# A token-major x product and a convolution summed by accumulating DMAs in layer A of a two-layer decoder

## The chip, the core and the metric

The kernel runs on one core of a Trainium2 chip. Its time is the device time of one execution in microseconds (us); for the kernel before it is the median of 3 runs, 1240.77 us, between 1240.29 and 1242.27. The engines are called PE (matmul; PEld is its weight load), DVE (vector), ACT (scalar, activation functions), POOL (GpSimd) and SP (the queue that issues nearly all DMAs). Each engine runs its own instructions strictly in their written order and waits at an instruction until what it needs is there.

## The reference, cut to what matters

256 tokens, model width 2048, all in float32. Layer A is a Mamba-2 mixer; layer B, dilated window attention, isn't touched. Of layer A this matters:

```python
h = x * (1.0 + scale) + shift                      # 256 x 2048, scale and shift from ada_w
z, xBC, dt = split(h @ in_w, [4096, 4096 + 6144])  # xBC: 4096 columns x, 1024 B, 1024 C
xBC = silu(causal_depthwise_conv(xBC, conv_w, conv_b))   # 4 taps: y[t] = sum_j w[j] * x[t-3+j] + b
xs, B, C = split(xBC)                              # 8 groups: 512 columns of x, 128 of B, 128 of C
y = ssd(xs * dt, dt * A, B, C) + xs * D_skip       # one chunk of 256 tokens
y = rms_norm(y * silu(z)) * norm_g @ out_w
```

## The kernel before, in words

Every product is made exact enough by splitting: a weight piece of 512 KB (`raw`, 128x1024) is loaded by SP into one of six buffers, ACT copies it to a rounded `whi` (L126), DVE subtracts to get the rest `wlo` (L127), four buffers each, and PE multiplies whi by the high and low halves of the activation and wlo by the high half. There are two forms. In `tm_mults` (L217 to L219) the activation is the stationary side and the result has tokens on partitions (token-major): per 128 rows of the weight, six matmuls of 512 columns. In `cm_part` (L176, L178) the weight is stationary and the result has channels on partitions (channel-major): per 128 rows and 512 channels, four matmuls of 512 columns and four of 256. During the startup `cm_piece` (L162 to L165) does the channel-major product with twelve matmuls of 256 columns, because the high and low halves of h come into being one after the other.

The startup loads 32 MB of `ada_w` to make scale and shift (L299), and h, 128 channels at a time; meanwhile PE works on pieces of products for which part of h exists. Ten products are begun that way and their partial sums parked in tiles (`begun`, L371). The products of x and of B and C of group 0 run through the whole startup in PSUM.

Then come the groups g = 0 to 7. `product` makes z (token-major), x and every second time B and C for two groups (channel-major). With channels on partitions the convolution (`conv`, L377) is shifts along the free axis: ACT multiplies by the last tap and adds the bias (L381), DVE adds three taps (L384), ACT applies Silu (L386). For x this is done on four tiles of 128 channels per group, after the two halves of each have been joined by ACT and DVE (L425, L426). `stage1` makes decay factors (`seg`: a broadcast load into `cbc`, Relu L687, Exp L690, product with the scores L691), turns the group's x into token-major with eight PE transposes into PSUM (L699), and lets DVE scale it by dt, D and the decay (L701, L704, L709). `stage2` multiplies on PE (L721, L729), adds and gates (L730, L731); `stage3` normalizes. Sixteen `ada_w` columns for the gate are worked off between pieces (L299).

The order on each engine isn't the written one: `arrange` lists the work by a model (`price`, `forward`, `backward`) and writes the order found into the program. The model prices every instruction, buffers and DMA; what it decides here is where in ACT's and DVE's queues the convolution's steps stand among the splits of the weight pieces.

Of the kernel before, what the change touches and what calls it, by code (L numbers as in the profile page):

```python
# [11 lines left out]
F32 = mybir.dt.float32  # L12
# [8 lines left out]
P = 128  # L21
# [27 lines left out]
WSUB = [("xs", g) for g in range(1, G)] + [("bc", g) for g in (2, 4, 6)]  # L49
# [22 lines left out]
def trunk(ctx, tc, xT, x, ada0, par, cst, bias, lnrow, ada, wdt, win, wsub, wout, wkv, wk, wbin, wbout, out):  # L72
# [278 lines left out]
    with ExitStack() as cA:  # L351
# [14 lines left out]
        with ExitStack() as cS:  # L366
# [5 lines left out]
                     ("xs", 1): (win[5], 4, as_cm(y[0])), ("bc", 2): (win[1], 4, as_cm(y[1])),  # L372
                     ("z", 2): (win[14], 14, y[2]), ("bc", 4): (win[2], 12, as_cm(y[5])), ("z", 4): (win[16], 6, y[4]),
                     ("z", 3): (win[15], 12, y[3]), ("z", 6): (win[18], 10, y[6]), ("z", 5): (win[17], 8, y[7])}
            xs, bc, sz = {}, {}, dict(enumerate(szt))
# [29 lines left out]
            def product(kind, g, pre=None):  # L405

                src, k0, part = begun.get((kind, g), (None, 0, None))
                if src is None:
                    src = win[{"bc": g // 2, "xs": 4 + g, "z": 12 + g}[kind]]
                if kind == "z":  # L410
                    ps = tm_chunk(src, hh_, hl_, rate=R, k0=k0, pre=pre)
                    if g not in sz:
                        sz[g] = p0.tile([P, 2, 512], F32, name="sz")
                    for b in range(2):
                        if part is not None:
                            V.tensor_tensor(part[:, b, :], ps[b], part[:, b, :], op=ALU.add)
                        S.activation(sz[g][:, b, :], part[:, b, :] if part is not None else ps[b], AF.Silu)
                    return
# [12 lines left out]
                if kind == "xs":  # L431
                    xs_conv(g, t)
                else:
                    bc_conv(g, t)

            with ExitStack() as c0:
# [58 lines left out]
                pss = {-2: first[0], -1: first[1]}  # L495
# [85 lines left out]
                for i, (k, q, ends) in enumerate(order):  # L581
# [8 lines left out]
                    z = str(k)[0] == "z"  # L590
# [38 lines left out]
                xs_conv(0, tiles(first[1]))  # L629
# [37 lines left out]
            def stage1(g):  # L667
# [11 lines left out]
                for w in range(2):  # L679
                    h0 = g * HPG + 4 * w  # L680
                    cbc = px.tile([P, 4, 2, P], F32, name="cbc")
                    nc.sync.dma_start(cbc, bass.AP(tensor=cumd.tensor, offset=cumd.offset + h0 * L,
                                                   ap=[[0, P], [L, 4], [P, 2], [1, P]]))
                    seg = px.tile([P, 4, 2, P], F32, name="seg")
                    for hh in range(4):
                        for b in range(2):
                            m = S.activation(seg[:, hh, b, :], cbc[:, hh, b, :], AF.Relu,  # L687
                                             bias=cumT[:, b, h0 + hh:h0 + hh + 1], scale=-1.0)
                            PINS.append((m.ins.name, early.ins.name))
# [5 lines left out]
                xd = px.tile([P, 2, 512], F32, name="xd", bufs=1)  # L695
                for b in range(2):
                    px_ = aux.tile([P, 512], F32, name="aux")
                    for i in range(4):
                        T.transpose(px_[:, i * P:i * P + P], xs[g][:, i, b * P:b * P + P], ident)  # L699
                    heads = px_.rearrange("p (h e) -> p h e", h=HPG)  # L700
                    V.tensor_tensor(xd[:, b, :].rearrange("p (h e) -> p h e", h=HPG), heads,  # L701
                                    dtT[:, b, g * HPG:(g + 1) * HPG, None].to_broadcast([P, HPG, 64]),
                                    op=ALU.mult)
                    V.tensor_tensor(y[g][:, b, :].rearrange("p (h e) -> p h e", h=HPG), heads,  # L704
                                    dskip[:, g * HPG:(g + 1) * HPG, None].to_broadcast([P, HPG, 64]),
                                    op=ALU.mult)
                    if b == 0:
                        xo = px.tile([P, 512], F32, name="xo", bufs=1)
                        V.tensor_tensor(xo.rearrange("p (h e) -> p h e", h=HPG), heads,  # L709
                                        dec[:, 0, g * HPG:(g + 1) * HPG, None].to_broadcast([P, HPG, 64]),  # L710
                                        op=ALU.mult)
# [474 lines left out]
def graph(ins):  # L1186

    nodes, tiles, live, lastpe = [], {}, {}, {}
    for x in ins:
# [3 lines left out]
        v.i, v.e = len(nodes), "SP" if "DMA" in type(x).__name__ else str(x.engine).split(".")[1]  # L1193
# [66 lines left out]
def build(ins, pools):  # L1260
# [9 lines left out]
    for x in ins:  # L1270
        if type(x).__name__ != "BassTilePoolBoundary":
            continue
        if x.name in byalloc:
# [13 lines left out]
            for tg, a, b, bufs in mine:  # L1287
                near = [(o, a < d and c < b or not tilewise) for kk, o, c, d in seen if kk == k and base < d and c < at]
                rng[tg] = (a, b, bufs, [o for o, full in near if full], [o for o, full in near if not full])
            held[p.id] = [(k, tg, a, b) for tg, a, b, bufs in mine]  # L1290
# [387 lines left out]
def _layout(x, c, ada_w, ada_b, ln_g, ln_b, a_in_w, a_conv_w, a_conv_b, a_dt_bias,  # L1678
# [4 lines left out]
    def put(name, a):  # L1683
# [43 lines left out]
        "wsub": _pieces(np.concatenate([xs[:, 512:], bc[:, 512:]], 1), 256, 4),  # L1727
# [24 lines left out]
```

## Time and profile before

| what | value |
|---|---|
| time, median of 3 runs | 1240.77 us |
| profiled execution, its span | 1238.4 us (the runs' median is 2.4 us above it) |
| PE busy | 1227.6 us, 99% of the span |
| DVE, ACT, POOL busy | 84%, 57%, 0% |
| DMA | 334.47 MB, 270 GB/s over the span |
| startup, the part at 420 GB/s | about the first 160 us |
| groups of layer A | about 160 to 520 us |

An engine's busy time counts an instruction from start to modelled end; matmuls overlap, so PE's pace is read from the distance between starts. In the grouped lines, "x64 | 11.0, 273 | 0.0" means 64 instructions, 11.0 us busy, 273 ns each, and 0.0 us of idle time just before them.

### The profile page before, as it was taken

The numbers are of one execution on the slowest core, as the hardware profiler recorded it, in microseconds if no ns is written. First come the engines' busy times: TensorE is split into PE (matmuls) and PEld (weight loads), VectorE is DVE, ScalarE is ACT, GpSimd is POOL, SyncE is SP. The second block draws the span as 40 slices with busy tenths as digits, with TensorE's granted clock in tenths as the row PEclk, the third lists the DMA queues.
The fourth block names the chain that finished last, engine by engine and source line by source line (L and its number), as shares of the span: only waits on it lengthen the run. The fifth ranks groups of instructions, "written<-read, shape, count | busy, mean of one in ns | idle before, by whom it ended". The sixth has DMA issues, their size and how long they took to land.

```text
span 1238.4 us, 18082 instructions
## 1 busy us (share of the span) xinstructions
PE 1227.6 (99%) x6712; PEld 1058.1 (85%) x6712; DVE 1035.9 (84%) x1481; ACT 703.1 (57%) x1054; POOL 0.2 (0%) x4
## 2 busy tenths in 40 slices
PE   8999999999999999999999999999999999999998
PEld 8889888888888888888888888888888888888886
DVE  6999998989999999978888699998865746757677
ACT  4655466768948589864335455444446644444561
POOL 0000000000000000000000000000000000000000
PEclk9999999999999999999999999999999999999999
DMA  9999977656696855748998669999985563551671
GB/s 368 422 422 421 422 271 241 223 189 234 263 339 224 318 182 190 245 154 294 384 386 308 233 221 369 412 377 378 353 308 187 200 192 103 168 182 64 203 285 68
DMA packets 81743, 334.47 MB, mean 270 GB/s; under 512 B 9108, under 2 KB 9844, under 8 KB 69496
## 3 DMA queue, kind: packets, MB, share of 16 engines
q1 hardware_dynamic: 81656, 333.33, 73.8%
q8 instruction: 52, 0.85, 0.3%
q14 instruction: 35, 0.29, 0.1%
HBM read 331.11 MB, written 2.18 MB: 269 GB/s over the span
## 4 chain that ended last, share of the span: by engine, by line
PE 86%; DMA 11%; DVE 2%; ACT 1%; issue 0%; SPq 0%; ACTq 0%
PE acc L176 27%; PE acc L178 14%; PE acc L217 12%; PE acc L218 12%; PE acc L219 12%; DMA raw<-in_win 8%; DMA araw<-in_ada 2%; PE py L729 2%; PE aux L993 1%; PE aux L699 1%; PE po L1017 1%; PE po L1006 1%; PE aux L994 1%; PE aux L721 1%; DMA y<-in_ada 1%; PE aux L783 0%
## 5 line engine op out<-in xcount | busy, mean ns | idle before, releaser
L126 ACT ACTIVATE whi<-raw 128x1024 fp32r<-128x1024 f32 (+1 forms) x393 | 409.7, 1049 | 342.2 <-PE acc L176 131.6
L127 DVE TENSOR_TENSOR wlo<-raw,whi 128x1024 fp32r<-128x1024 f32 (+1 forms) x393 | 471.2, 1211 | 119.2 <-ACT whi L126 113.3
L176 PE MATMUL acc<-act,whi 128*128 128x512 f32 x1456 | 376.8, 395 | 0.0
L176 PEld LDWEIGHTS acc<-act,whi 128*128 128x128 f32 x1456 | 262.5, 188 | 45.7
L218 PE MATMUL acc<-wlo,act 128*128 128x512 f32 x672 | 257.0, 393 | 0.2 <-DVE wlo L127 0.2
L217 PE MATMUL acc<-whi,act 128*128 128x512 f32 x672 | 249.4, 395 | 1.3 <-ACT whi L126 0.7
L299 DVE SCALAR_TENSOR_TENSOR araw<-araw,cb__72 128x2048 f32<-128x2048 f32 x92 | 210.3, 2285 | 7.0 <-DMA araw<-in_ada 6.7
L178 PE MATMUL acc<-act,wlo 128*128 128x256 f32 x1456 | 212.1, 284 | 0.0
L178 PEld LDWEIGHTS acc<-act,wlo 128*128 128x128 f32 x1456 | 200.4, 190 | 13.5 <-issue 0.5
L219 PE MATMUL acc<-whi,act 128*128 128x512 f32 x432 | 163.0, 392 | 0.0
L218 PEld LDWEIGHTS acc<-wlo,act 128*128 128x128 f32 x672 | 126.0, 188 | 27.1 <-DVE wlo L127 1.1
L217 PEld LDWEIGHTS acc<-whi,act 128*128 128x128 f32 x672 | 125.3, 188 | 27.8 <-ACT whi L126 1.2
L219 PEld LDWEIGHTS acc<-whi,act 128*128 128x128 f32 x432 | 81.1, 188 | 16.7 <-issue 0.7
L219 PE MATMUL acc<-whi,ylo 128*128 128x512 f32 x240 | 89.8, 392 | 0.0
L219 PEld LDWEIGHTS acc<-whi,ylo 128*128 128x128 f32 x240 | 45.0, 188 | 9.3 <-DVE ylo L789 0.2
L164 PE MATMUL acc<-act,whi 128*128 128x256 f32 x208 | 51.6, 284 | 0.8 <-ACT whi L126 0.4
L165 PE MATMUL acc<-act,wlo 128*128 128x256 f32 x208 | 51.9, 284 | 0.0
L162 PE MATMUL acc<-act,whi 128*128 128x256 f32 x208 | 42.0, 284 | 0.0
L164 PEld LDWEIGHTS acc<-act,whi 128*128 128x128 f32 x208 | 38.0, 191 | 2.4 <-ACT whi L126 0.6
L687 ACT ACTIVATE seg<-cbc,cumT 128x128 f32<-128x128 f32 x128 | 39.8, 389 | 0.0
L165 PEld LDWEIGHTS acc<-act,wlo 128*128 128x128 f32 x208 | 38.1, 191 | 0.8
L384 DVE SCALAR_TENSOR_TENSOR cacc<-ct,prm,cacc 128x255 f32<-128x255 f32 (+2 forms) x84 | 36.2, 477 | 1.0 <-ACT cacc L381 0.9
(269 smaller groups left out, 1147.1 us busy)
## 6 DMA issues: line engine op xcount, KB each, us to landing
araw<-in_ada SPq DMA_DIRECT2D x92, 1024.0 KB, 7.3
raw<-in_win SPq DMA_DIRECT2D x86, 512.0 KB, 9.8
raw<-in_wsub SPq DMA_DIRECT2D x70, 512.0 KB, 4.4
raw<-in_wout SPq DMA_DIRECT2D x64, 512.0 KB, 5.2
raw<-in_wbin SPq DMA_DIRECT2D x64, 512.0 KB, 3.4
raw<-in_wkv SPq DMA_DIRECT2D x48, 512.0 KB, 4.7
raw<-in_wk SPq DMA_DIRECT2D x48, 512.0 KB, 6.7
cbc<-cumd SPq DMA_DIRECT2D x16, 512.0 KB, 5.0
```

The source lines that it names most:

```text
L126: a = S.activation(hi[:, c_], raw[:, c_], AF.Copy)
L127: m = V.tensor_tensor(lo[:, c_], raw[:, c_], hi[:, c_].bitcast(F32), op=ALU.subtract)
L162: T.matmul(o, hi[:, k, c_], alo[:, kt, :], start=False, stop=kt == k1 - 1, skip_group_check=True)
L164: note("product", T.matmul(o, hi[:, k, c_], ahi[:, kt, :], start=kt == k0 and n % 2 == 0, stop=False, skip_group_check=True))
L165: T.matmul(o, lo[:, k, c_], ahi[:, kt, :], start=False, stop=False, skip_group_check=True)
L176: T.matmul(ps[n], hi[:, k, c_], both[:, kt], start=first, stop=False, skip_group_check=True)
L178: T.matmul(ps[n][:, 0, :], lo[:, k, c_], high[:, kt, :], start=first, stop=False, skip_group_check=True)
L217: begin = T.matmul(ps[b], h_, hi[:, k, :], start=kt == k0, stop=False)
L218: T.matmul(ps[b], h_, lo[:, k, :], start=False, stop=False)
L219: end = T.matmul(ps[b], l_, hi[:, k, :], start=False, stop=kt == k1 - 1)
L299: V.scalar_tensor_tensor(raw, raw, 1.0, cb_, op0=ALU.mult, op1=ALU.mult, accum_out=to)
L687: m = S.activation(seg[:, hh, b, :], cbc[:, hh, b, :], AF.Relu, bias=cumT[:, b, h0 + hh:h0 + hh + 1], scale=-1.0)
```

## The change

The x product becomes token-major (`tm_chunk` instead of `cm_wide`; in the startup `tm_piece` instead of `cm_piece`), so its result already lies as `stage1` wants it, and the eight transposes per group go. A shift by one token is now a shift of one partition, which DVE and ACT can't do. So `xs_conv` lets DVE multiply the result by four rows of taps, broadcast over the partitions (`crow`, a new 1 MB load per group): three products into `tap0` to `tap2` and the last one into `y[g]`, for both blocks b of 128 tokens. DMAs issued by POOL then add `tap2` one row lower into `y[g]`, `tap1` two rows lower, `tap0` three rows lower, the rows that cross from block 0 to block 1, and the bias row: eleven accumulating DMAs per group. Each that adds to a row of `y[g]` waits until the one before it has landed. One Silu on ACT ends it. `stage1` reads x from `y[g]`. The separate `cbc` tile goes (the load goes into `seg`), partial sums are parked elsewhere, and the model prices a POOL DMA with 1.0 us on its queue and 3.2 us to landing.

```diff
-            def xs_conv(g, t):
-                xs[g] = p0.tile([P, 4, L], F32, name="xs")
-                for i in range(4):
-                    conv(t[i], 4 * g + i, xs[g][:, i, :])
+            def xs_conv(g, ps):
+                w = p0.tile([P, 4, 512], F32, name="crow", bufs=1)
+                rows = crow.offset + g * 5 * 512
+                nc.sync.dma_start(w, bass.AP(tensor=crow.tensor, offset=rows, ap=[[0, P], [512, 4], [1, 512]]))
+                taps = []
+                for b in range(2):
+                    taps.append([p0.tile([P, 512], F32, name=f"tap{j}", bufs=2) for j in range(3)])
+                    for j in range(3):
+                        V.tensor_tensor(taps[b][j], ps[b], w[:, j, :], op=ALU.mult)
+                    V.tensor_tensor(y[g][:, b, :], ps[b], w[:, 3, :], op=ALU.mult)
+                def add(dst, src):
+                    nc.gpsimd.dma_start(dst, src, accum_op=ALU.add)
+                for b in range(2):
+                    for j in (2, 1, 0):
+                        o = 3 - j
+                        add(y[g][o:, b, :], taps[b][j][:P - o])
+                        if b:
+                            add(y[g][:o, b, :], taps[0][j][P - o:])
+                    add(y[g][:, b, :], bass.AP(tensor=crow.tensor, offset=rows + 4 * 512, ap=[[0, P], [1, 512]]))
+                S.activation(y[g], y[g], AF.Silu)
...
+                if kind == "xs":
+                    ps = tm_chunk(src, hh_, hl_, rate=R, k0=k0)
+                    if part is not None:
+                        for b in range(2):
+                            V.tensor_tensor(part[:, b, :], ps[b], part[:, b, :], op=ALU.add)
+                        ps = [part[:, b, :] for b in range(2)]
+                    xs_conv(g, ps)
+                    return
...
-            z = str(k)[0] == "z"
+            z = k == -1 or str(k)[0] in "zx"
...
                 for b in range(2):
-                    px_ = aux.tile([P, 512], F32, name="aux")
-                    for i in range(4):
-                        T.transpose(px_[:, i * P:i * P + P], xs[g][:, i, b * P:b * P + P], ident)
-                    heads = px_.rearrange("p (h e) -> p h e", h=HPG)
+                    heads = y[g][:, b, :].rearrange("p (h e) -> p h e", h=HPG)
...
+    if e == "Pool" and "DMA" in type(x).__name__:
+        return 1.0, 3.2, None, 0
```

The order moves on all engines. On PE, before, the transposes of a middle group stand between two z pieces (L217 to L219) and the x product that follows is channel-major (L176):

```order
L699 MATMUL aux_2818<-cc_74,xs_2143 128x128 x4
L217 MATMUL acc_2834<-whi_2838,act1_86 128x512
L218 MATMUL acc_2834<-wlo_2839,act1_86 128x512
L219 MATMUL acc_2834<-whi_2838,act1_86 128x512
...
L699 MATMUL aux_2827<-cc_74,xs_2143 128x128 x3
L217 MATMUL acc_2835<-whi_2838,act1_86 128x512
L699 MATMUL aux_2827<-cc_74,xs_2143 128x128
...
L176 MATMUL acc_2904<-act0_85,whi_2908 128x512
```

After, no transposes are left there, and the x product of group 6 (into acc_4012 and acc_4013) is token-major; with its last piece, whi_4143, it hands over to z:

```order
L217 MATMUL acc_4013<-whi_4143,act1_86 128x512
L219 MATMUL acc_4012<-whi_4143,act1_86 128x512
L218 MATMUL acc_4013<-wlo_4144,act1_86 128x512
L219 MATMUL acc_4013<-whi_4143,act1_86 128x512
L219 MATMUL acc_4233<-whi_4236,act1_86 128x512
```

What moved: x products have the instructions of z products, and the convolution follows on DVE as soon as acc_4012 is complete. On ACT, before, the four Silus of a group's x stand one by one among the splits, each behind DVE's three tap additions (here that of the first 128 channels, between two splits of weight pieces):

```order
L126 ACTIVATE whi_4704<-raw_4702 128x1024
L381 ACTIVATE cacc_4595<-ct_4483,prm_73 128x256
L425 ACTIVATE ct_4582<-acc_4486 128x256
L425 ACTIVATE ct_4585<-acc_4487 128x256
...
L126 ACTIVATE whi_4774<-raw_4772 128x1024
L386 ACTIVATE xs_4588<-cacc_4589 128x256
```

After, ACT has one Silu for group 6 (L417), between the splits whi_4414 and whi_4432, the eighth and the ninth piece that PE takes after whi_4143:

```order
L126 ACTIVATE whi_4414<-raw_4412 128x1024
L417 ACTIVATE y6_96<-y6_96 128x1024
L126 ACTIVATE whi_4432<-raw_4430 128x1024
L126 ACTIVATE whi_4450<-raw_4448 128x1024
L126 ACTIVATE whi_4468<-raw_4466 128x1024
```

What moved: every split from whi_4432 on now stands behind a Silu that waits for all eleven DMAs of the group. POOL had no work before; after, this is its whole part for group 6 (names as above, `in_crow` is the bias row):

```order
L408 DMA y6_96<-tap2_4169 127x512
L408 DMA y6_96<-tap1_4168 126x512
L408 DMA y6_96<-tap0_4167 125x512
L408 DMA y6_96<-in_crow 128x512
L408 DMA y6_96<-tap2_4176 127x512
L408 DMA y6_96<-tap2_4169 1x16x32
L408 DMA y6_96<-tap1_4175 126x512
L408 DMA y6_96<-tap1_4168 2x512
L408 DMA y6_96<-tap0_4167 3x512
L408 DMA y6_96<-tap0_4174 125x512
L408 DMA y6_96<-in_crow 128x512
```

What moved: the first four belong to block 0, the rest to block 1, and the second, third and fourth of block 0 each wait for the landing of the one before; so do 126, 125 and the bias of block 1. On SP, the startup's queue of loads has one more entry, early (before: the same place without it):

```order
L118 DMA raw_235<-in_win 128x1024
L278 DMA araw_209<-in_ada 128x2048
L399 DMA crow_1716<-in_crow 128x2048
L118 DMA raw_271<-in_win 128x1024
L278 DMA araw_220<-in_ada 128x2048
```

What moved: everything behind crow_1716 is loaded 1 MB later.

More of the change, by code (lines that the diff above doesn't have):

```diff
@@ L48 @@
 NKEY = 768
-WSUB = [("xs", g) for g in range(1, G)] + [("bc", g) for g in (2, 4, 6)]
+WSUB = [("bc", g) for g in (2, 4, 6)]
 CD, CA, NBIAS = 0, NKEY, 2 * NKEY
@@ L1192, in graph @@
         v = Node()
-        v.i, v.e = len(nodes), "SP" if "DMA" in type(x).__name__ else str(x.engine).split(".")[1]
+        v.i, v.e = len(nodes), str(x.engine).split(".")[1]
         v.occ, v.lat, v.tab, v.nb = price(x, v.e)
```

53 lines of the change are left out of this document (24 added, 29 removed).

## The prediction

> **What bounds the kernel now.** I read the page first: busy shares, slices, chain.
>
> ```profile
> PE 1227.6 (99%) x6712; PEld 1058.1 (85%) x6712; DVE 1035.9 (84%) x1481; ACT 703.1 (57%) x1054; POOL 0.2 (0%) x4
> ...
> PE 86%; DMA 11%; DVE 2%; ACT 1%; issue 0%; SPq 0%; ACTq 0%
> PE acc L176 27%; PE acc L178 14%; PE acc L217 12%; PE acc L218 12%; PE acc L219 12%; DMA raw<-in_win 8%; DMA araw<-in_ada 2%; PE py L729 2%; PE aux L993 1%; PE aux L699 1%; PE po L1017 1%; PE po L1006 1%; PE aux L994 1%; PE aux L721 1%; DMA y<-in_ada 1%; PE aux L783 0%
> ```
>
> PE is at work for 99% of the span and is 86% of the chain, so what comes off PE comes off the time, unless PE then waits; the next largest part, 11%, is DMA. Next the stretches (PE, PEld, DVE, ACT, POOL busy, clock, DMA share, GB/s): one of the startup, then three of the groups' stage.
>
> ```profile
> 100.00:150.00 50.00, 50.00 (x324) 45.76 (x323) 47.72 (x52) 24.75 (x30) 0.00 (x0) 1.00 1.02 422
> 160.00:195.00 35.00, 34.82 (x175) 29.67 (x175) 32.29 (x62) 23.50 (x37) 0.00 (x0) 1.00 0.64 214
> 350.00:400.00 50.00, 50.00 (x274) 42.96 (x272) 48.37 (x71) 33.40 (x60) 0.00 (x0) 1.00 0.76 272
> 400.00:450.00 50.00, 49.98 (x292) 43.71 (x292) 50.00 (x81) 30.55 (x49) 0.00 (x0) 1.00 0.72 255
> ```
>
> In the startup the DMA engines are full at 422 GB/s and PE is filled with begun products. In the groups' stage DMA has room, PE is full, and DVE nearly so: what comes late on ACT or DVE there is soon late on PE. The waits say which transfer leads; the first row is of 20 to 160 us, the second of 160 to 520:
>
> ```profile
> ACT whi L126 <- DMA raw<-in_win: 49.8, 37, 4.6
> ```
> ```profile
> ACT whi L126 <- PE acc L176: 30.1, 25, 2.9
> ```
>
> So in the startup ACT waits for weight pieces; later it runs ahead and waits for PE to give buffers back.
>
> **What PE loses.** PE's pace is the distance between starts. From the timeline: four transposes and what follows; then ten starts of a token-major product (the nine between are left out), and stage 2's matmuls; from the chain, sixteen starts each of the channel-major forms.
>
> ```profile
> 304.47 0.60 PE L699 MATMUL aux<-cc,xs 128*128 128x128 f32 x4
> 304.82 0.48 PE L217 MATMUL acc<-whi,act 128*128 128x512 f32 x1
> 305.14 0.40 PE L218 MATMUL acc<-wlo,act 128*128 128x512 f32 x1
> ...
> 307.90 0.39 PE L218 MATMUL acc<-wlo,act 128*128 128x512 f32 x1
> ...
> 310.17 0.39 PE L219 MATMUL acc<-whi,act 128*128 128x512 f32 x1
> 310.40 1.02 PE L721 MATMUL aux<-xo,cb 128*128 128x512 f32 x2
> 311.25 1.00 PE L729 MATMUL py<-xd,seg 128*128 128x64 f32 x8
> 312.06 0.48 PE L176 MATMUL acc<-act,whi 128*128 128x512 f32 x1
> ```
> ```profile
> 257.62 1.91 PE acc L178 x16
> 259.53 3.65 PE acc L176 x16
> ```
>
> (310.17 - 307.90) / 10 = 0.227 us per 512 columns. The transposes take 304.47 to 304.82, and the next matmul 0.32 instead of 0.227: 0.44 for four, 0.11 each. All 64 go (L699's group below has them): -7.0 us. Channel-major costs per 128 weight rows 4 x (3.65 + 1.91) / 16 = 1.390, token-major 6 x 0.227 = 1.362; 108 such steps (six groups of 16, and 12 that the startup leaves of group 1) give 108 x 0.03 = -3.2. Together -10.2, all on PE and so all on the path.
>
> **The startup.** The row of group 0's taps is 128x2048 floats, 1.05 MB, early in a queue that is full: 1.05 / 0.422 = +2.5 us for all behind it. In the other direction 20 steps of 12 matmuls at 1.91 / 16 become 6 at 0.227: 20 x 0.07 = -1.4, which counts only where PE leads. With ACT 49.8 us in wait for pieces DMA leads, so I take +2.5; bounds -1.4 and +2.5.
>
> **DVE and ACT.** These rows carry it:
>
> ```profile
> L699 PE MATMUL aux<-cc,xs 128*128 128x128 f32 x64 | 11.0, 273 | 0.0
> L384 DVE SCALAR_TENSOR_TENSOR cacc<-ct,prm,cacc 128x255 f32<-128x255 f32 x28 | 12.9, 478 | 0.9 <-ACT cacc L381 0.9
> L381 ACT ACTIVATE cacc<-ct,prm 128x256 f32<-128x256 f32 x28 | 16.1, 594 | 1.1 <-DVE ct L426 0.6
> L425 ACT ACTIVATE ct<-acc 128x256 f32<-128x256 f32 x28 | 9.8, 374 | 8.0 <-PE acc L176 5.5 <-DVE cacc L384 2.4
> L426 DVE TENSOR_TENSOR ct<-acc,ct 128x256 f32<-128x256 f32 x28 | 11.0, 415 | 3.5 <-ACT ct L425 3.5
> L386 ACT ACTIVATE xs<-cacc 128x256 f32<-128x256 f32 x32 | 12.5, 410 | 4.5 <-DVE cacc L384 4.4
> L731 DVE TENSOR_TENSOR y<-y,sz 128x512 f32<-128x512 f32 x16 | 10.9, 684 | 0.0
> L690 ACT ACTIVATE seg<-seg 128x1024 f32<-128x1024 f32 x16 | 16.8, 1058 | 0.2
> L126 ACT ACTIVATE whi<-raw 128x1024 fp32r<-128x1024 f32 x385 | 405.0, 1058 | 333.0 <-PE acc L176 131.6 <-PE acc L219 128.1 <-DMA raw<-in_win 45.2
> L127 DVE TENSOR_TENSOR wlo<-raw,whi 128x1024 fp32r<-128x1024 f32 x385 | 465.8, 1221 | 118.5 <-ACT whi L126 112.5 <-PE acc L178 3.0 <-issue 0.9
> ```
>
> Per group DVE drops 4 x 0.415 + 12 x 0.478 = 7.4 and gains eight 128x512 products, 8 x 0.684 = 5.5; ACT drops 4 x (0.374 + 0.594 + 0.410) = 5.5 and gains one Silu of 128x1024, 1.06 by the nearest row. Off PE: 0. The products of stage 1 (dt, D, decay) are the same five and read SBUF, not PSUM; 128x512 from SBUF is L731's row: 0. `seg` loads without `cbc` start later; the later group's Relu finds six raw buffers, 16 us of pieces, ahead of it: 0, and some 5 us per group if that fails. The seven later 1 MB tap loads meet a DMA share of 0.64 to 0.76: 0, or 2.5 each without that room.
>
> **The new wait.** Silu of group g stands in ACT's queue and waits for eleven DMAs; behind it are the splits of the weight pieces, and behind them PE. The additions to the same rows follow one another, each issued when the last has landed. On the longest way that makes seven steps: three of block 0; then block 1's first, issued behind block 0's bias, and its 126 rows, 125 rows and bias (group 0, whose small rows come later: eight). No run here shows such a DMA; these issues bound its step (KB each, then median us from issue to landing; then all sixteen of `cbc`, with the issue itself in ns).
>
> ```profile
> out<-u SPq DMA_DIRECT2D x8, 256.0 KB, 2.4
> gt<-gated SPq DMA_DIRECT2D x4, 256.0 KB, 5.7
> cbc<-cumd SPq DMA_DIRECT2D x16, 512.0 KB, 5.0
> ```
> ```profile
> L682 SPq DMA_DIRECT2D cbc<-cumd x16: 326/327/424, 206.0 to 478.0; - x16
> ...
> DMA to landing us min/median/max: 3.3/5.0/7.4
> ```
>
> Stores of the same 256 KB at the kernel's empty end take 2.4. In the very stage 512 KB take 3.3 at best and 5.0 at the median; less the 256 KB too many (0.6 at 422 GB/s) that is 2.7 and 4.4. I take 3.1, near the lower: POOL's DMAs have a queue of their own, but must read the destination too and share the engines. Ends: 2.4 and 4.4 (5.7 behind a full queue). Three issues that nothing waits out add 1.0 (at SP's 0.33 each, an estimate). A group's chain: 7 x 3.1 + 1.0 = 22.7.
>
> The Trainium skill (DMA: Bandwidth & Descriptors, Anatomy of one DMA — SWDGE) gives for a DMA issued from GpSimd 2.0 us plus the bytes at 436 GB/s, an estimate of 2.6 for these; the step would then make waits of 7 instead of the 28 below, and the whole 1240, 1 us under the time before. No trace here has such a DMA; the stage's own best row, 2.7, lies above it.
>
> What hides the chain, for group 6: between the x product's last matmul of block 0 and PE's first use of whi_4432 the order has 90 matmuls of 512 columns, one L739 (before: L721, two in 0.85) and sixteen of 64 columns (eight in 0.81): 20.4 + 0.43 + 1.6 = 22.4. Of that DVE takes 4 x 0.684 = 2.7 before the first DMA can go, and Silu 1.06, one product by the decay 0.68 and the split 1.22 come after the last: 3.0. Room 16.7, chain 22.7: PE waits 6.0.
>
> Counted so, groups 0 to 7 have room for 23.9, 20.4, 14.8, 20.2, 19.4, 21.2, 16.7 and 19.8. (Groups 0, 1, 4: DVE does the products behind other work, so I count from the split before them and give it one piece of lead, 12 x 0.227 = 2.7. Group 2: DVE meets the decay product one piece before ACT meets Silu.) Waits: 1.9 (eight steps), 2.3, 7.9, 2.5, 3.3, 1.5, 6.0, 2.9: **28 us**. At a step of 2.4: 4; at 2.7: 9; at 4.0: 80; at 4.4: 102.
>
> **Sum.** -7.0 - 3.2 + 2.5 + 28 = +20: span 1238.4 to 1259, and with the 2.4 us between the profiled span and the runs' median, 1240.8 to **1261**. The sign turns at a step of about 2.65 us.
>
> **Rivals.**
> - *The chain hides.* Steps at the store's 2.4 us make 17.8, and all groups but 2 and 6 have room: waits of 4, so -7.7 + 4 gives 1237; with no wait at all 1233. For it: four weight buffers and ACT's 57%; a wait on ACT of less than PE's stock costs nothing. Against: the stage's DMAs were never under 3.3. Chance 0.37.
> - *Odd row counts don't spread.* 127 rows aren't divisible over 16 engines. If one engine moves them all, it does so at 422 / 16 = 26 GB/s: 9.9 us instead of 0.6, twice per chain, and 125 rows on five engines cost 1.3 more, twice: +21 per group, 170 in all, 1261 + 170 = 1431. All rows here have 128, 64 or 16 partitions, so nothing speaks for or against. Chance 0.08. The Trainium skill (DMA: Bandwidth & Descriptors, Why a DMA increments its semaphore by 16 and not by 1) says that the number of engines is the largest divisor up to 16 of the slowest dimension, 1 for 127, but that some direct copies from GpSimd were seen to spread over 16; no run here shows which holds for an addition.
> - *Traffic.* Eleven DMAs that read source and destination, and 1 MB of taps, are some 5 MB per group of 45 us, 115 GB/s beside 213 to 273, under the 422 that the startup shows. If weight pieces come late nevertheless, say one of 2.7 per group: -7.7 + 8 x 2.7 = +14, 1255. Chance 0.05.
> - That the transposes stay, or that the x product keeps its form, the order rules out.
>
> **Chances.** The forecast (steps of 2.7 to 4) has 0.50; its own range is 1242 to 1313. A measurement here can tell 0.2%, 2.5 us. Faster: 0.32 of the rival that hides the chain. Same: its other 0.05 and 0.04 of the forecast. Slower: 0.46 + 0.08 + 0.05 = 0.59. The range takes in the hidden chain, 1233, and a step of 4, 1312; outside lie the unspread rows and slower steps.
>
> **What would show it.** Right: POOL's DMAs into y land in about 3.1 us; ACT's L417 waits for DMA in every group, most in 2 and 6, some 5 to 10 us in the timeline; PE loses 20 to 35 us there; no L699 on `xs`; the startup ends 2 to 3 us later. Wrong: steps under 2.6 us, or PE without gaps though ACT waits (then splits lay further ahead than I counted); or landings of 10 us for 127 rows.

## The result and the profile after

The changed kernel takes 1449.4 us (median of 4 runs, 1446.7 to 1451.1) where the kernel before takes 1240.7 on the same chip: a ratio of 1.168, 95% interval 1.166 to 1.170. The forecast was 1261 with a range up to 1312: the direction was right, the size was not, by a factor of ten in the loss (+209 us instead of +20).

From the page of the changed kernel: busy times and TensorE's granted clock, the chain that ended last (the page accounts for 65% of it), and two of the costliest groups in which waits for the convolution show (busy, mean ns, then idle time before them and what ended it).

```profile
PE 1245.7 (86%) x6312; PEld 1049.7 (72%) x6312; DVE 1028.5 (71%) x1419; ACT 672.0 (46%) x972; POOL 75.7 (5%) x92
...
PEclk9999996888779786979699999999999999999999
...
PE 52%; DMA 5%; issue 3%; ACT 2%; DVE 2%; POOL 1%; ACTq 0%; POOLq 0%; DVEq 0%
...
L217 PE MATMUL acc<-whi,act 128*128 128x512 f32 x928 | 353.1, 404 | 92.0 <-ACT whi L126 91.1
...
L417 ACT ACTIVATE y<-y 128x1024 f32<-128x1024 f32 x8 | 8.4, 1056 | 153.2 <-DMA y<-in_crow 153.2
```

PE was 99% busy and is 86%. The clock, at full speed before, drops in slices between 7 and 20, which are the groups' stage. ACT idles 153 us in front of Silu's own instruction (L417), in six waits. The waits of the groups' stage, 160 to 750 us (us in total, times, longest), show the rest, and how this reaches PE:

```profile
POOL y L408 <- DMA y<-tap: 244.9, 48, 11.2
ACT y L417 <- DMA y<-in_crow: 153.2, 6, 31.7
...
PE acc L217 <- ACT whi L126: 90.4, 4, 23.5
...
ACT L417 <- DMA y<-in_crow: 56.9, 2, 29.7
...
ACT L417 <- DMA y<-tap: 25.9, 1, 25.9
```

GpSimd waits for each addition before it issues the next, and Silu for the last of them. The two rows "ACT L417" are waits in front of an instruction that loads Silu's table (ACT_TABLE_LOAD, of the same line) and stands ahead of Silu in three groups; with them ACT waits 236 us in all eight groups. In seven groups PE then waits for the split of a weight piece that is queued on ACT behind Silu (L126, or the rest L127 that DVE makes from it); in the eighth it waits for DVE's product by the decay (L725), which reads Silu's result. The second group's chain on GpSimd, from its timeline (start, duration, idle time before it and what ended it; x2 is a large addition and the small carry beside it):

```profile
248.71 0.86 POOL L408 DMA_DIRECT2D y<-tap  x1 [21.46 <-DVE y L405]
254.91 0.84 POOL L408 DMA_DIRECT2D y<-tap  x1 [5.34 <-DMA y<-tap]
265.01 0.84 POOL L408 DMA_DIRECT2D y<-tap  x1 [9.26 <-DMA y<-tap]
272.76 0.89 POOL L408 DMA_DIRECT2D y<-in_crow  x1 [6.91 <-DMA y<-tap]
273.31 2.04 POOL L408 DMA_DIRECT2D y<-tap  x2
281.89 1.67 POOL L408 DMA_DIRECT2D y<-tap  x2 [6.54 <-DMA y<-tap]
286.18 1.71 POOL L408 DMA_DIRECT2D y<-tap  x2 [2.62 <-DMA y<-tap]
290.84 0.90 POOL L408 DMA_DIRECT2D y<-in_crow  x1 [2.95 <-DMA y<-tap]
```

The steps are the seven of the prediction, but they are 6.2, 10.1, 7.8, 8.6 (block 1's first, beside the bias), 4.3 and 4.7 us apart, not 3.1. The chain runs 46.3 us from the first issue to the last landing. The first ones meet weight pieces on their way; the last ones come when PE and the loads stand still, and are the shortest.

The page's DMA issues (KB each, median us from issue to landing):

```profile
y<-in_crow POOLq DMA_DIRECT2D x16, 256.0 KB, 4.3
y<-tap POOLq DMA_DIRECT2D x16, 254.0 KB, 5.9
y<-tap POOLq DMA_DIRECT2D x16, 252.0 KB, 4.3
y<-tap POOLq DMA_DIRECT2D x16, 250.0 KB, 5.1
```

Over all 64 large additions the mean is 5.93 us. I sorted them by how many loads were under way (issued, not landed) at their issue: with none, 27 of them, the median is 3.99 us; with one 4.55; with two 6.4; with three or more 7.4 to 8.4.

Last, the clock. Stretches around the first stall (PE, PEld, DVE, ACT, POOL busy, granted clock, DMA share, GB/s), then PE's timeline at its end:

```profile
213.00:216.00 3.00, 0.08 (x1) 0.00 (x0) 0.00 (x0) 0.00 (x0) 0.00 (x0) 1.00 0.65 201
217.00:234.00 17.00, 0.00 (x0) 0.00 (x0) 1.29 (x2) 3.36 (x4) 4.53 (x6) 0.50 0.33 46
234.00:240.00 6.00, 5.01 (x11) 3.64 (x12) 5.64 (x7) 3.17 (x5) 0.00 (x0) 0.50 0.52 171
241.00:248.00 7.00, 7.00 (x32) 5.79 (x32) 6.96 (x10) 6.00 (x17) 0.00 (x0) 1.00 1.00 385
```
```profile
234.24 0.79 PE L217 MATMUL acc<-whi,act 128*128 128x512 f32 x1 [21.15 <-ACT whi L126]
...
237.66 0.63 PE L219 MATMUL acc<-whi,act 128*128 128x512 f32 x1
238.08 0.63 PE L217 MATMUL acc<-whi,act 128*128 128x512 f32 x1
...
240.84 0.39 PE L219 MATMUL acc<-whi,act 128*128 128x512 f32 x1
241.06 0.39 PE L217 MATMUL acc<-whi,act 128*128 128x512 f32 x1
```

PE stands from 213 to 234. Three microseconds into the stall the granted clock falls to half, and it stays there until 6 us after PE is back: matmuls of 512 columns then start 0.43 us apart instead of 0.227.

There are eight stalls, one in each group, of 21.2, 24.9, 25.1, 22.5, 23.2, 22.6, 23.5 and 21.1 us: 184 us. What matmuls lose at half clock outside the stalls adds 28 us. Together that is 212 of the 211 us between the two spans; what comes off PE and some 8 us more in short pauses about cancel.

### The profile page after: what moved, and what is told of

Same layout as the page of the kernel before. It is cut to its first block, busy times and chain, and to the rows that moved or that the text cites. A ratio compares the mean times of both kernels' runs of the same rounds, so it can differ in the third digit from the quotient of the medians.

```text
span 1449.3 us, 17353 instructions
## 1 busy us (share of the span) xinstructions
PE 1245.7 (86%) x6312; PEld 1049.7 (72%) x6312; DVE 1028.5 (71%) x1419; ACT 672.0 (46%) x972; POOL 75.7 (5%) x92
## 3 DMA queue, kind: packets, MB, share of 16 engines
q0 software_dynamic: 9984, 16.69, 7.6%
## 4 chain that ended last, share of the span: by engine, by line
PE 52%; DMA 5%; issue 3%; ACT 2%; DVE 2%; POOL 1%; ACTq 0%; POOLq 0%; DVEq 0%
PE acc L176 14%; PE acc L218 9%; PE acc L217 9%; PE acc L219 9%; PE acc L178 7%; DMA y<-tap 4%; DMA y<-in_crow 1%; POOL y L408 1%; ACT whi L126 1%; ACT seg L711 1%; DVE wlo L127 1%; PE py L747 1%; PE aux L801 1%; PE po L1035 0%; PE aux L1011 0%
## 5 line engine op out<-in xcount | busy, mean ns | idle before, releaser
L127 DVE TENSOR_TENSOR wlo<-raw,whi 128x1024 fp32r<-128x1024 f32 (+1 forms) x393 | 471.7, 1210 | 203.3 <-ACT whi L126 195.9
L126 ACT ACTIVATE whi<-raw 128x1024 fp32r<-128x1024 f32 (+1 forms) x393 | 407.7, 1048 | 329.8 <-PE acc L219 147.1
L217 PE MATMUL acc<-whi,act 128*128 128x512 f32 x928 | 353.1, 404 | 92.0 <-ACT whi L126 91.1
L218 PE MATMUL acc<-wlo,act 128*128 128x512 f32 x928 | 362.9, 402 | 28.2 <-DVE wlo L127 28.2
L176 PE MATMUL acc<-act,whi 128*128 128x512 f32 x1024 | 270.7, 399 | 24.9 <-ACT whi L126 24.9
L217 PEld LDWEIGHTS acc<-whi,act 128*128 128x128 f32 x928 | 177.3, 192 | 132.9 <-ACT whi L126 93.7
L219 PE MATMUL acc<-whi,act 128*128 128x512 f32 x688 | 263.0, 397 | 0.0
L218 PEld LDWEIGHTS acc<-wlo,act 128*128 128x128 f32 x928 | 177.5, 192 | 70.2 <-DVE wlo L127 33.4
L176 PEld LDWEIGHTS acc<-act,whi 128*128 128x128 f32 x1024 | 186.1, 190 | 57.6 <-ACT whi L126 25.3
L178 PE MATMUL acc<-act,wlo 128*128 128x256 f32 x1024 | 150.7, 285 | 22.6 <-DVE wlo L127 22.6
L178 PEld LDWEIGHTS acc<-act,wlo 128*128 128x128 f32 x1024 | 142.1, 192 | 31.9 <-DVE wlo L127 22.8
L219 PEld LDWEIGHTS acc<-whi,act 128*128 128x128 f32 x688 | 131.6, 191 | 26.6 <-issue 0.2
L408 POOL DMA_DIRECT2D y<-tap x72 | 63.3, 1001 | 546.0 <-DVE y L405 321.7
L219 PE MATMUL acc<-whi,ylo 128*128 128x512 f32 x240 | 91.2, 396 | 0.2 <-DVE ylo L807 0.2
L725 DVE TENSOR_TENSOR xo<-y,dec 128x512 f32<-128x512 f32 x8 | 5.5, 687 | 105.0 <-ACT y L417 105.0
L417 ACT ACTIVATE y<-y 128x1024 f32<-128x1024 f32 x8 | 8.4, 1056 | 153.2 <-DMA y<-in_crow 153.2
L219 PEld LDWEIGHTS acc<-whi,ylo 128*128 128x128 f32 x240 | 45.4, 190 | 9.9 <-DVE ylo L807 0.9
L711 ACT ACTIVATE seg<-seg,cumT 128x128 f32<-128x128 f32 x128 | 39.6, 389 | 1.1 <-DMA seg<-cumd 1.1
```

The source lines that it names most:

```text
L126: a = S.activation(hi[:, c_], raw[:, c_], AF.Copy)
L127: m = V.tensor_tensor(lo[:, c_], raw[:, c_], hi[:, c_].bitcast(F32), op=ALU.subtract)
L176: T.matmul(ps[n], hi[:, k, c_], both[:, kt], start=first, stop=False, skip_group_check=True)
L178: T.matmul(ps[n][:, 0, :], lo[:, k, c_], high[:, kt, :], start=first, stop=False, skip_group_check=True)
L217: begin = T.matmul(ps[b], h_, hi[:, k, :], start=kt == k0, stop=False)
L218: T.matmul(ps[b], h_, lo[:, k, :], start=False, stop=False)
```

## The experiments

Three theories stood at the start. **A**: the serial steps are slow (latency, and weight pieces on the same DMA engines), and Silu waits for all of them. **B**: row counts of 127, 126 and 125 do not spread over the engines. **C**: the planner, told 1.0 us a step, merely put Silu and what follows too early. **D** was that the loss lies in another part of the change.

**1. no_sums.**
```diff
-                for b in range(2):
-                    for j in (2, 1, 0):
...
-                    add(y[g][:, b, :], bass.AP(tensor=crow.tensor, offset=rows + 4 * 512, ap=[[0, P], [1, 512]]))
                 S.activation(y[g], y[g], AF.Silu)
```


> Leaves out all accumulating DMAs of the convolution (tap products stay and are not summed, no bias), the rest as in the changed kernel. Theory A, slow serial steps (each of the seven serial steps of a group takes 4.4 us when no weight piece is queued and 6 to 10 us when some are, and Silu stands behind all of them): the whole loss goes, and what is left is my -10.2 on TensorE and +2.5 at the start, 1233 us (1229 to 1240). Theory B, odd row counts (127, 126 and 125 rows are not spread over all DMA engines): the same. Theory D, the loss sits elsewhere (the crow loads, seg without cbc, the new z6 buffer, y as a buffer of the partial sums): it stays over 1300 us.

Measured 1234.3 us, 0.995 of before (0.993 to 0.997). From its page:
```profile
PE 1218.0 (99%) x6312; PEld 1036.4 (84%) x6312; DVE 1024.7 (83%) x1419; ACT 674.1 (55%) x972; POOL 0.2 (0%) x4
```
PE is full again and there is no stall. D falls; the additions are the whole loss, 215 us. It also tests the rest of the sum: -10.2 + 2.5 = -7.7 was counted, -6.3 (in the medians; -7.8 in the spans) was measured.

**2. nowait.** The same additions go into a tile that nobody reads.
```diff
-                    for j in (2, 1, 0):
+                    for j, s in ((2, 2), (1, 1), (0, 2)):
                         o = 3 - j
-                        add(y[g][o:, b, :], taps[b][j][:P - o])
+                        add(taps[b][0][o:], taps[b][s][:P - o])
...
-                    add(y[g][:, b, :], bass.AP(tensor=crow.tensor, offset=rows + 4 * 512, ap=[[0, P], [1, 512]]))
+                    add(taps[b][0], bass.AP(tensor=crow.tensor, offset=rows + 4 * 512, ap=[[0, P], [1, 512]]))
```


> The same 17 accumulating DMAs for a group, of the same sizes and in the same serial chains, but into the tap0 tiles, which nobody reads: Silu works on unsummed products, so the convolution is left out. Theory A: TensorE no longer stalls, and the time is 1233 to 1245 us; since weight pieces now flow all the time, the steps are long throughout, 6 to 10 us each, with none at 4.4. If the DMAs cost by their traffic (they slow the weight pieces), the time stays over 1260 us. Theory B: no stalls either, and steps as in the changed kernel whatever is queued, 4 to 6 us by row count.

Measured 1302.4 us (1.050, 1.049 to 1.052): far over A's 1245, and where the traffic theory had put it (over 1260). But the waits of VectorE give another cause:
```profile
DVE tap L404 <- DMA tap<-tap: 32.4, 6, 7.6
...
DVE tap L404 <- DMA tap<-in_crow: 18.2, 4, 5.9
```
The chains, now 42 to 57 us, are longer than a group's 45 us of PE work, so the next group's tap products wait 50.6 us for their buffers, and PE has gaps of 46 us in all. With nobody waiting for the sums the chain still comes through, by way of its buffers. The large steps land in 6.8 us on average, more than the 5.9 of the changed kernel: less standing still means more weight pieces beside them (18 of the 64 find no load under way, where it was 27).

**3. rows112.**
```diff
-                        add(y[g][o:, b, :], taps[b][j][:P - o])
+                        add(y[g][:112, b, :], taps[b][j][:112])
                         if b:
-                            add(y[g][:o, b, :], taps[0][j][P - o:])
+                            add(y[g][112:, b, :], taps[0][j][112:])
...
```


> Each accumulating DMA moves 112 rows without a shift (the bias too, carries are 16 rows): a multiple of 16 in place of 127, 126 and 125 rows. The sums are not the convolution. Theory B, odd row counts: the steps fall to the 4.3 us of the 128-row bias step or below, and the kernel falls by 100 us or more, under 1350 us. Theory A: a step loses only its bytes, an eighth of a burst of 2.2 to 4 us, 0.3 to 0.5 us; seven steps and eight groups make 17 to 28 us at most: 1420 to 1449 us.

Measured 1431.6 us (1.154, 1.152 to 1.156), inside A's range. The issues of this kernel:
```profile
y<-tap POOLq DMA_DIRECT2D x48, 224.0 KB, 4.9
```
With no load under way 112 rows take 3.63 us at the least; in the changed kernel 125, 126, 127 and 128 rows take 3.87, 3.93, 3.99 and 3.92 at the least. The packets say the same: in the probe below a quiet addition of 127 rows is 127 packets of 2 KB and some small writes of 4 and 8 bytes, and all are through 2.2 us after the first starts, like those of 128 rows in the changed kernel (2.0 to 2.3). B falls.

**4. told.** The planner is given the step's landing, and that an addition reads its destination.
```diff
-        return 1.0, 3.2, None, 0
+        return 1.0, 5.2 if list(o.ap)[0][1] > 3 else 3.6, None, 0
...
-        for a, w in [(a, False) for a in _aps(x.ins)] + [(a, True) for a in _aps(x.outs)]:
+        for a, w in [(a, False) for a in _aps(x.ins) + (_aps(x.outs) if v.e == "Pool" else [])] + [(a, True) for a in _aps(x.outs)]:
```


> The same program, but the planner that orders it is told that an accumulating DMA lands after 5.2 us (3.6 for one to three rows) and that it reads what it adds to, so that a serial step is spaced by its landing and not by 1.0 us. The TensorE work from a group's last product to the weight piece behind its Silu grows from 15 to 24 us to 31 to 55 us. Theory A: a chain of 40 to 45 us then overhangs by 0 to 12 us in five or six groups: 1260 to 1300 us, and the half clock behind stalls mostly goes. Theory C, the planner's price alone made the loss and there is enough other work: 1245 us or less. If the loss is in something that order cannot change: over 1400 us.

Measured 1320.1 us (1.063, 1.061 to 1.065): 129 us come back with the same DMAs in another order of the work around them, but less than A expected. Its waits from 160 to 760 us:
```profile
POOL y L408 <- DMA y<-tap: 161.2, 44, 8.6
...
ACT y L417 <- DMA y<-in_crow: 33.3, 4, 12.3
...
ACT L417 <- DMA y<-in_crow: 26.0, 4, 11.8
```
ACT's wait for the sums, in front of Silu and of its table, falls from 236 to some 60 us. The large steps grow, though, from 5.9 to 7.7 us on average. The steps at 4 us in the changed kernel came when the kernel stood still and no load was under way.

**5. pairs and pairs_pin.** Both blocks' additions of one tap go together, so that four pairs stand in series.
```diff
-                for b in range(2):
-                    for j in (2, 1, 0):
-                        o = 3 - j
+                for j in (2, 1, 0):
+                    o = 3 - j
+                    for b in range(2):
                         add(y[g][o:, b, :], taps[b][j][:P - o])
-                        if b:
-                            add(y[g][:o, b, :], taps[0][j][P - o:])
+                    add(y[g][:o, 1, :], taps[0][j][P - o:])
```


> The same accumulating DMAs, bytes and rows, and the same sums, in another order: GpSimd takes one tap of both blocks before the next tap, so that four pairs stand in series where seven or eight single steps did. Theory A (serial latency of the steps): a pair takes a single step and 1 to 2 us more, 6 to 7 us with pieces queued, the chain 24 to 28 us where it was 40 to 46, and each group gains about 17 us of wait and part of 3.5 us at half clock: 1449 - 8 x 18 = 1305 us (1270 to 1340). If the accumulating traffic itself were the limit (bytes through the engines), the order would change nothing: 1430 us or more.

Measured 1442.6 us (1.162, 1.160 to 1.164). This looks like a verdict against A, and is none: GpSimd's timeline still has block 0's three taps and bias, one behind the other, ahead of block 1's first.
```profile
247.67 0.86 POOL L408 DMA_DIRECT2D y<-tap  x1 [19.93 <-DVE y L405]
252.24 0.84 POOL L408 DMA_DIRECT2D y<-tap  x1 [3.71 <-DMA y<-tap]
257.38 0.84 POOL L408 DMA_DIRECT2D y<-tap  x1 [4.29 <-DMA y<-tap]
267.48 0.89 POOL L408 DMA_DIRECT2D y<-in_crow  x1 [9.25 <-DMA y<-tap]
268.02 2.04 POOL L408 DMA_DIRECT2D y<-tap  x2
```
The planner sorts GpSimd's queue too, and put the old order back. So once more with the order pinned:
```diff
+                    if chain:
+                        PINS.append((m.ins.name, chain[-1].ins.name))
+                    chain.append(m)
```


> Tap by tap for both blocks once more, now with the order on GpSimd pinned; without the pins the planner put the first block's whole chain ahead again, since by its price of 1.0 us a step that chain was done before the second block's products. Four pairs in series. Theory A (serial latency): a pair takes 6 to 8 us where seven or eight steps of 4 to 10 us stood, the chain 26 to 32 us instead of 40 to 46, and the kernel comes to 1310 to 1360 us. If the traffic of the accumulating DMAs sets the time, it stays at 1430 us or more.

Measured 1373.8 us (1.108, 1.105 to 1.110): 76 us less than the changed kernel with the same bytes, 14 us above A's range. The chains are 28 to 39 us where 26 to 32 was expected, since here too the steps are longer, 7.3 us on average. That the traffic alone sets the time is out.

**6. half.**
```diff
-                        add(y[g][o:, b, :], taps[b][j][:P - o])
+                        add(y[g][o:, b, :256], taps[b][j][:P - o, :256])
...
```


> Each accumulating DMA covers half the columns (1 KB of each row), the other half stays unsummed. Theory A (a step is mostly latency and waiting behind weight pieces): in a quiet queue a step lands in about 3.0 us where the 127 rows of 2 KB take 3.99, and behind pieces it loses no more; seven or eight steps in eight groups save 45 to 65 us: 1385 to 1405 us. If bytes set the step, the chain halves: about 1290 us. If only the number of descriptors does, nothing changes: 1440 to 1449 us.

Measured 1399.2 us (1.127, 1.125 to 1.129), as A expected. The issues of the three taps:
```profile
y<-tap POOLq DMA_DIRECT2D x16, 127.0 KB, 4.7
y<-tap POOLq DMA_DIRECT2D x16, 126.0 KB, 3.0
y<-tap POOLq DMA_DIRECT2D x16, 125.0 KB, 3.1
```
Half the bytes take 0.85 us off the mean step (5.08); seven steps in eight groups make 48 of the 50 us gained. With no load under way an addition of a tap lands in 2.8 to 3.0 us, 1.1 less than with all the bytes. The packets show what is left: at rest the first starts 1.4 us after the issue in both kernels, and all are through 1.2 us later here, 2.2 in the changed kernel. So of its 3.9 to 4.0 us some 1.7 do not depend on the bytes.

**7. tree and tree_told.** The same sums in two serial steps; VectorE adds the bias (and the bc convolution's `cacc` goes from three buffers to one).
```diff
-                w = p0.tile([P, 4, 512], F32, name="crow", bufs=1)
+                w = p0.tile([P, 5, 512], F32, name="crow", bufs=1)
...
+                    V.tensor_tensor(y[g][:, b, :], y[g][:, b, :], w[:, 4, :], op=ALU.add)
...
+                for s, d in ((0, [t[1] for t in taps]), (2, [y[g][:, b, :] for b in range(2)])):
+                    for b in range(2):
+                        add(d[b][1:], taps[b][s][:P - 1])
+                    add(d[1][:1], taps[0][s][P - 1:])
+                for b in range(2):
+                    add(y[g][2:, b, :], taps[b][1][:P - 2])
+                add(y[g][:2, 1, :], taps[0][1][P - 2:])
```


> The same convolution with two serial steps in place of seven or eight: tap0 is added to tap1 shifted by one row while tap2 is added to y shifted by one row, then that tap1 is added to y shifted by two rows; all six large DMAs of a step pair run for both blocks together, and VectorE adds the bias row (a fifth row of the crow tile; the bc convolution's cacc tile keeps one buffer to make room). Theory A: the chain is 15 to 18 us, inside the 15 to 24 us of TensorE work that stand before the weight piece behind Silu: 1236 to 1260 us. If each group's stall has another cause than the chain's length, it stays above 1300 us.

Measured 1341.3 us (1.080, 1.078 to 1.082), 108 less than the changed kernel and 81 above A's range. GpSimd's timeline for one group:
```profile
401.84 0.85 POOL L409 DMA_DIRECT2D tap<-tap  x1 [26.64 <-DVE tap L404]
406.42 1.66 POOL L409 DMA_DIRECT2D tap<-tap  x2 [3.73 <-DVE tap L404]
422.41 0.83 POOL L409 DMA_DIRECT2D y<-tap  x1 [14.33 <-DVE cb L702]
429.60 2.57 POOL L409 DMA_DIRECT2D y<-tap  x3 [6.35 <-DMA y<-tap]
```
GpSimd waits 14 us for VectorE before the additions into y (the row names L702, which ends just then): all products are done at 408.5 us, but VectorE adds the bias row (L406), new in this version, only at 421.3 and 425.4, behind splits and other work. It looks as if the planner, at 1.0 us a step, saw no hurry in it. The next run changes only the planner: the price, and, as in told, that an addition reads its destination.
```diff
-        return 1.0, 3.2, None, 0
+        return 1.0, 6.0 if list(o.ap)[0][1] > 3 else 6.0, None, 0
```

> The tree with an honest price in the planner: each accumulating DMA lands after 6.0 us and reads what it adds to. Theory A: nothing is left of the stalls, 1233 to 1245 us, level with the kernel before or up to 0.6% below it. Theory C (order matters more than the chain): clearly below the tree with the old price, by 10 us or more.

Measured 1273.1 us (1.027, 1.025 to 1.029): 68 us from what the planner is told alone, so C is a true part of the loss; but 28 us above A's range.

**8. told8 and tree_told8** ask for how much the price still counts, with 8.0 us for the 5.2 and 6.0 of the two runs above.
```diff
-        return 1.0, 5.2 if list(o.ap)[0][1] > 3 else 3.6, None, 0
+        return 1.0, 8.0 if list(o.ap)[0][1] > 3 else 4.0, None, 0
```

> As the run with the planner told 5.2 us a step, now with 8.0 us (4.0 for one to three rows), near what the steps took there behind weight pieces. Theory A: more TensorE work is put between products and Silu, the stalls of 3 to 12 us shrink, 1265 to 1300 us; a rest stays, since a chain of seven steps of 8 us is longer than a group's own 45 us of TensorE work and the tap tiles have to come free for the next group. If the order has nothing more to give: 1310 to 1325 us.

Measured 1287.2 us (1.036, 1.032 to 1.040), inside the range.

```diff
-        return 1.0, 6.0 if list(o.ap)[0][1] > 3 else 6.0, None, 0
+        return 1.0, 8.0 if list(o.ap)[0][1] > 3 else 8.0, None, 0
```


> The tree of two serial steps, with the planner told 8.0 us instead of 6.0. Theory A: the stalls left there (16 us, and 15 us at half clock) go, 1240 to 1262 us. If what is left does not hang on the price of a step: 1268 to 1278 us, as with 6.0.

Measured 1257.0 us (1.013, 1.010 to 1.016), inside the range. The page has PE at 98%, and from its waits of 160 to 760 us:
```profile
PE 1225.9 (98%) x6312; PEld 1033.6 (83%) x6312; DVE 1035.5 (83%) x1435; ACT 685.3 (55%) x980; POOL 60.8 (5%) x76
```
```profile
ACT seg L712 <- DMA seg<-cumd: 12.6, 6, 3.5
...
ACT L418 <- DMA y<-tap: 4.2, 2, 2.2
...
ACT y L418 <- DMA y<-tap: 2.5, 2, 1.5
```
Of the stalls one gap of 2.8 us is left, and ACT waits 6.7 us for the sums. The span is still 22 us over that of no_sums. The largest part of it, 14 us, is in pauses under 2.5 us between matmuls (starts at least 0.15 us later than the median distance of their form: 32.5 us in all, 18.6 in no_sums). How much of them the sixteen further VectorE additions, the traffic of the DMAs, the later `seg` loads (the first row; 1.9 us in no_sums) and the order make was not tried apart.

**9. probe.** A step by itself: no_sums without the tap products, and fifty additions that nobody waits for.
```diff
+        probe = [pa.tile([P, 512], F32, name=f"probe{i}") for i in range(2)]
+        for t in probe:
+            V.memset(t, 0.0)
+        for _ in range(50):
+            nc.gpsimd.dma_start(probe[0][1:], probe[1][:P - 1], accum_op=ALU.add)
```


> The convolution's sums and its tap products are left out, and fifty accumulating DMAs of 127 rows run one behind the other from the kernel's start into a tile of their own, from a tile of zeros; no engine waits for them. It measures one step by itself under the weight traffic of a TensorE that never stalls. Theory A: 7 to 10 us a step as long as three or more weight pieces are under way, and never near 3.1; the fifty steps last 350 to 500 us. The kernel stays near the one without sums, 1232 to 1240 us: what the change pays is the wait, not the traffic. If the traffic counts, it is 1250 us or more. If a step is 4.0 us here too, the long steps of the changed kernel come from something other than the weight pieces.

Two rows of its timeline in the startup, two at 300 us, and the median of all fifty from its DMA issues:
```profile
120.24 0.84 POOL L360 DMA_DIRECT2D probe<-probe  x1 [7.79 <-DMA probe<-probe]
128.97 0.85 POOL L360 DMA_DIRECT2D probe<-probe  x1 [7.89 <-DMA probe<-probe]
...
301.07 0.87 POOL L360 DMA_DIRECT2D probe<-probe  x1 [5.98 <-DMA probe<-probe]
305.37 0.85 POOL L360 DMA_DIRECT2D probe<-probe  x1 [3.43 <-DMA probe<-probe]
```
```profile
probe<-probe POOLq DMA_DIRECT2D x50, 254.0 KB, 8.0
```
The step is as A said: 8.2 us at the median (19 steps) with seven loads under way in the startup, 4.0 in the best cases of the groups' stage, never 3.1. Beside the seven loads its first packet starts 4.0 us after the issue (1.4 at rest), and the packets take 3.8 us (2.2 at rest). The loads make this and not PE's work: the step at 301.07 us lands in 3.95 us with PE busy at full clock throughout, while the DMA engines move only 75 GB/s. The time is not as A said: 1267.8 us (1.022, 1.020 to 1.023), 33 us over no_sums. The startup's last channel-major matmul (L162) starts at 195.7 instead of 165.2 us, 30 us later; from there to the end of the groups only 4 us are lost. Traffic of additions is dear where the DMA engines are full, and cheap in the groups' stage.

## Why the prediction was wrong, point by point

- **What comes off PE and the startup (-10.2, +2.5).** Right as a sum: -7.7 counted, -6.3 measured without the sums. The transposes of `xs` are gone (the 16 of L699 left are of `bcm`). The startup's +2.5 was not tried apart, but its size shows: the last rows of scale and shift (`mod`, L317 on DVE) come at 159.5 us before, and at 161.9 in the changed kernel, 2.4 us later.
- **Off PE: 0.** No contradiction: with the sums left out PE is at 99%, with the new DVE products and Silu in place. `seg<-cumd` landed in 8.9 us at the median where `cbc` had 5.0, and the Relu behind it waited 1.1 us in all (L711); where the kernel stalls less it waits more, 12.6 us in the tree at 8.0 us.
- **The place of the wait.** Right: ACT at L417 in every group, splits behind it, PE behind those in seven of the eight, seven serial steps. The rooms held too: the eight chains of 39.5 to 46.8 us add to 351.7; less the rooms, 156.4 in all, that is 195 us; the stalls measured are 184.
- **The step, 3.1 us: the term that failed.** Measured 5.93 on average. Put into the prediction's own table, 7 x 5.93 + 1.0 = 42.5 a group, 190 us of waits instead of 28. Two errors in it. The floor was too low: with no load under way an addition takes 3.87 to 3.99, not the 2.4 to 2.7 that I read from stores and from loads less their bytes; at 4.0 my table already gave 80 us. And the upper end was too low: I ended at 4.4 and put the 5.7 of a full queue aside, but three or more loads under way make it 7.4 to 8.4, and the probe shows that a PE which does not stall keeps such loads coming. My "POOL's DMAs have a queue of their own" was true (the page lists one, with 16.69 MB) and did not help: beside loads the steps are still twice as long.
- **Not counted: the clock.** Each stall costs 2.1 to 3.8 us more at half clock behind it, 22 us, and a ninth stretch at half clock, 718 to 732 us, just behind the last stall, some 6: 28 us. 1240.8 - 7.7 + 190 + 28 = 1451, against 1449.4.
- **Not counted: the planner's price.** I took the rooms from its order and treated them as given. They were a consequence of its 1.0 us on the queue and 3.2 to landing, without the read of the destination; told that read, and 5.2 or 8.0 us, it makes them longer, and 129 and 162 us of the loss go. The changed kernel's +209 is the change and a price that hides it from the planner.
- **Rivals.** The chain that hides needed steps of 2.65; the shortest of the large ones took 3.87. Odd row counts: settled by rows112 and the packets, no effect. The Trainium skill (DMA: Bandwidth & Descriptors, Why a DMA increments its semaphore by 16 and not by 1) has both the rule by which 127 rows would take one engine and the exception for GpSimd's direct copies; the trace agrees with the exception for additions: 127 rows land like 128 (3.99 and 3.92 us), though which engines take the packets it does not tell. The Trainium skill's formula for a DMA issued from GpSimd (DMA: Bandwidth & Descriptors, Anatomy of one DMA — SWDGE), from which I had an estimate of 2.6 us, does not agree: 3.9 at best here. Traffic: not the loss in this kernel, but real in the startup (probe).
- **The range.** It ended at a step of 4.0, just where the measured floor lies. The bounds came from DMAs of another kind (no read of the destination, another issuer), and I kept the range narrow as if they were of the same. It names slower steps as lying outside, yet gives them none of the chances, which add to 1 without them.

No version here beats the kernel before. Without any sums there are 6 us to gain, and the best version with the whole convolution, 1257 us, is 23 us above that.

## What to carry to other kernels

A chain of dependent DMAs is priced by its length times the landing that a like transfer has while loads are under way (7 to 8 us here); the quiet floor, 4 us here, is mostly seen once the kernel has stalled. Before a wait is costed by an order that a planner made, ask by what price it made it: give it the true one, or the new operation gets no cover, and an edit of the code's order may be undone. A long stall of PE is paid twice, in time and in clock: in the runs here half clock followed every pause of PE over 3 us, and some of those between 1 and 3.

## What the runs showed of the hardware

- **An accumulating DMA of 254 KB inside SBUF** lands in 4.0 us when no load is under way, in 2.9 to 3.0 at half the bytes, in 8.2 beside seven loads. It does not wait for all of those: in the probe, from 19 to 181 us, two to five of the loads issued before each addition are still not landed when it lands, and 2.5 to 3.1 MB of loads move meanwhile. So both queues are served side by side. The Trainium skill (DMA: Bandwidth & Descriptors, Queues, rings and completion order) says that the engines take the queues in turn, packet by packet; the trace agrees as far as this goes.
- **Additions in a full startup** cost more than their bytes: 23 of them, 6.0 MB, are 15 us at 411 GB/s; the startup became 30 us longer. That source and destination are both read would explain a factor of two; it was not tried.
- **Half clock behind a gap.** In the changed kernel it began 2 to 5 us into each of the eight stalls and ended 4 to 7 us after PE was back; in the tree at 8.0 us a gap of 2.8 us was enough for 3.4 us of it, and the stretch at 718 us began in a pause of 1.6 us. The Trainium skill (TensorE: Matmul & The Clock Gate, Part 1: The HAM clock gate) has a free-running window of about 3.4 us and a half clock after an idle one; the lengths here, 13.7, 20.5, 23.9 and 27.3 us, are multiples of it, so the trace agrees on the window; on what counts as an idle one it does not, since the pauses of 2.8 and 1.6 us are shorter.
